# A 1-core decoder layer: first norm from a features-first copy of the tokens, gating bias on ScalarE, and other SBUF places around the output projection

## The chip, the core and the metric

The kernel runs on one core of a Trainium2 chip. The metric is the device time of one execution in microseconds (us). Engines are named as in the profile: PE (TensorE, matmul), PEld (its weight loads), DVE (VectorE), ACT (ScalarE), POOL (GpSimd), SP (SyncE, which here only issues DMA transfers).

## What is computed

One layer of a decoder serves a prompt group of 512 tokens and a sample group of 64 tokens (8 sequences of 8), with D = 1024:

```python
z = rmsnorm(x, ln1_g) @ w_in            # q, kv (4 streams), window kv, gates, u|v
o_a = nsa_mixer(q, kv, window, gates)   # compressed + selected + window attention
o_b = gelu(u) * (w_s @ layernorm(gelu(v)) + b_s)   # per 128 positions, w_s lower triangular
h = x + concat(o_a, o_b) @ w_out
y = rmsnorm(h + relu(rmsnorm(h, ln2_g) @ w_ff1)**2 @ w_ff2, ln_f_g)

def rmsnorm(x, g):
    y = x * rsqrt(mean(x * x, axis=-1) + EPS)
    return y * g
```

The prompt group attends to itself. Each sample sequence attends to a paged cache of 1024 earlier positions and to 512 window rows, which a page table and a state array supply. The new key, value and window rows are outputs too, and so is the window state shifted by 8 rows.

## The kernel before, in words

All matrix products run in float32r with both operands split in a high and a low part (`split`, L104 to L107: ACT copies the high part, DVE or POOL subtracts it to get the low one). A product is then three products (high by high, high by low, low by high). The 64 sample tokens stand as high and low part beside each other in one 128-column operand (`AST`, `Hst`), so that two products are enough. `load_unit` (L136 to L141) loads 128 x 512 of a weight matrix into a `raw` tile and splits it into a unit `wu`. Tokens come in five tiles: t = 0 to 3 are the prompt's, 128 rows each, t = 4 is the sample's 64 rows.

The program is staged, and a tile framework orders each engine's instructions by priorities and dependences; SP issues all DMA transfers in one order, and a transfer behind a waiting one waits with it. The stages and their place in the profiled span:

- **First norm and key/value projection**, 0 to 45 us (L306 to L328). For each token tile: load the rows, sum of squares (ACT), inverse root `rstd` (DVE and POOL, L143 to L148), scaled rows `xn` (DVE), eight PE transposes through PSUM, a split into `AH` and `AL`; for the sample tile into `AST`. Then 24 products of that tile (16 for the sample) into one PSUM bank `pd`, over the eight units of `w_in` columns 512 to 1023, and its evacuation `ev_kv` (L260).
- **Gating values and compressed keys**, 45 to 78 us: columns for v, five banks side by side, and the compression of the prompt's keys (`pc`).
- **Window keys, gates, spatial gating, queries**, 78 to 120 us. `psg` (L489 to L494) holds the mixed values; DVE adds the bias `bsc` out of PSUM, four times 128 x 512. `wsT` is copied out of PSUM by DVE (L455). `evac_q` (L506 to L521) scales the queries by 0.125 and splits them to `Q`, ACT and DVE straight from PSUM.
- **Prompt attention**, 120 to 240 us, with query (`pq`) and u (`pu`) products as filler between its steps.
- **Sample attention**, 240 to 354 us, in four pairs of sequences, 0 to 3. A pair's 16 cached pages (16 x 256 KB) are a tile `G` (`load_pages`, L624). For a pair: compressed keys (`pcs`, PE products over `G`), window scores (`w_a`, `w_b`), selected scores (`s`), the softmax on ACT and DVE (`soft`), compressed values (`pcs` again), and then the values (`values`: transposes `tp` of the probabilities, products `o` over `VB`, `G` and `W`, a last transpose `to`). `values` of a pair runs inside the next pair's turn. There are three buffers for four pairs: pair 3's pages are loaded into pair 0's buffer as soon as pair 0's values have been formed (`load_pages(3, gps[0])` at `pr == 1`, L917). After that SP issues eight copies of window state to the output, HBM to HBM (`out_wins`, L926).
- **Output projection and second norm**, 354 to 422 us: the attention result `OTp` (features first) is split into `Hh` and `Hl`, 16 units of `w_out` are loaded and split, `out_proj` (L970 to L983) forms t = 0 to 3 for each half of the columns and then the sample tile, the result is added to the residual `R[t]`, and `norm_transpose` (L150) makes the next operand. The places in SBUF for `Hh`, `Hl`, `raw` and the units (pools L931 to L947) lie over the tiles of the sample attention, and the five PSUM banks of `acc` over its banks.
- **FFN**, 422 to 810 us, and the last norm to 829 us.

## Time and profile before

| what | value |
|---|---|
| device time, median of 3 runs | 832.47 us (831.67 to 832.74) |
| the profiled execution, its own time | 831.24 us |
| its span | 829.0 us |
| busy PE, DVE, ACT, POOL | 793.0, 444.6, 347.2, 175.0 us |
| mean PE clock granted | 0.991 of full speed |

An engine's busy time is the time in which it had an instruction in work; waits and DMA issues are not counted. The span is the profiled stretch, 2.2 us less than the time of that execution. A line of the chain of work names what the end of the program waited for at that moment, followed back from the last instruction. "<-DVE xn" in an idle time's brackets says who ended it.

### The profile page before, as it was taken

The page shows a single profiled execution, that of the slowest core. Times are in us where ns is not written, and L with a number is a line of the kernel's source. Part 1 is how long each engine was busy: PE and PEld are TensorE (multiplying, and loading weights), DVE is VectorE, ACT ScalarE, POOL GpSimd, SP SyncE. Part 2 cuts the span into 40 slices and gives each one's busy share as a digit, 9 for nine tenths or more (in the row PEclk, how much of TensorE's full clock was granted, in tenths as well). Part 3 has the DMA queues.
Part 4 walks back from the last instruction along what each step waited for, and adds up shares of the span by engine and source line. Part 5 has one row for each costly group of instructions (what it writes and reads, how often), then busy time and mean ns, then how long its engine had stood idle before and what let it go on. Part 6 is the DMA issues. An engine that isn't in the chain of part 4 may idle for free.

```text
span 829.0 us, 13177 instructions
## 1 busy us (share of the span) xinstructions
PE 793.0 (96%) x4855; PEld 687.2 (83%) x4855; DVE 444.6 (54%) x972; ACT 347.2 (42%) x856; POOL 175.0 (21%) x219
## 2 busy tenths in 40 slices
PE   5999999999999999799999999999999999999996
PEld 4788978878776777578888998989989899898985
DVE  4553978899864423474746245163452634435325
ACT  5444467888753232451734242242322323232213
POOL 2001844454210011140212010111111111111112
PEclk9999999999999999999999999999999999999998
DMA  8561420100698167193334132141320413302003
GB/s 265 169 194 35 127 62 14 39 2 1 235 334 271 43 213 226 30 284 118 119 111 141 64 99 63 44 153 51 102 88 15 154 51 102 102 16 99 1 1 114
DMA packets 54178, 90.20 MB, mean 109 GB/s; under 512 B 7618, under 2 KB 18850, under 8 KB 53986
## 3 DMA queue, kind: packets, MB, share of 16 engines
q1 hardware_dynamic: 53858, 89.30, 34.0%
q8 instruction: 38, 0.62, 0.3%
q14 instruction: 26, 0.21, 0.1%
q0 software_dynamic: 256, 0.07, 0.0%
HBM read 85.08 MB, written 8.39 MB: 113 GB/s over the span
## 4 chain that ended last, share of the span: by engine, by line
PE 85%; DVE 5%; DMA 3%; ACT 3%; issue 1%; SPq 1%; POOL 1%; POOLq 0%; ACTq 0%; DVEq 0%
PE acc L95 52%; PE pd L95 7%; PE pcs L95 6%; PE o L95 4%; PE pu L95 3%; PE s L95 3%; PE tp L685 2%; PE pq L95 2%; DMA raw<-in_w_in 2%; PE pc L95 1%; DVE wu L107 1%; DVE y L1034 1%; DMA G<-in_cache_kv 1%; ACT Hh L106 1%; ACT wu L106 0%
## 5 line engine op out<-in xcount | busy, mean ns | idle before, releaser
L95 PE MATMUL acc<-Hh,wu 128*128 128x288 f32 x1024 | 206.0, 296 | 0.0
L106 ACT ACTIVATE wu<-raw 128x512 fp32r<-128x512 f32 (+1 forms) x184 | 105.9, 614 | 157.8 <-PE acc L95 119.7
L95 PEld LDWEIGHTS acc<-Hh,wu 128*128 128x128 f32 x1024 | 165.3, 189 | 0.6 <-ACT Hh L106 0.2
L95 PE MATMUL acc<-wu,Fh 128*128 128x512 f32 x512 | 155.5, 389 | 0.0
L95 PE MATMUL acc<-Hl,wu 128*128 128x288 f32 x512 | 151.2, 296 | 0.0
L107 DVE TENSOR_TENSOR wu<-raw,wu 128x512 fp32r<-128x512 f32 x160 | 110.2, 730 | 53.5 <-ACT wu L106 53.5
L95 PEld LDWEIGHTS acc<-wu,Fh 128*128 128x128 f32 x512 | 95.7, 188 | 19.5
L95 PE MATMUL acc<-wu,Fl 128*128 128x512 f32 x256 | 97.1, 389 | 0.0
L95 PEld LDWEIGHTS acc<-Hl,wu 128*128 128x128 f32 x512 | 96.4, 188 | 0.3
L1055 DVE TENSOR_TENSOR f<-relu 128x576 f32<-128x576 f32 x32 | 24.2, 756 | 118.8 <-ACT relu L1054 118.8
L958 DVE TENSOR_TENSOR R<-acc,R 128x512 f32<-128x512 f32 x72 | 47.6, 687 | 62.8 <-PE acc L95 62.6
L1054 ACT ACTIVATE relu<-acc 128x288 f32<-128x288 f32 x64 | 26.1, 408 | 117.8 <-PE acc L95 117.8
L964 POOL TENSOR_TENSOR R<-atm,R 64x512 f32<-64x512 f32 x18 | 30.5, 1701 | 155.0 <-DVE atm L963 148.6
L1057 POOL CAST Fst<-Fh 128x64 fp32r<-128x64 f32 x32 | 23.5, 734 | 176.5 <-ACT Fh L106 119.7
L95 PE MATMUL pcs<-G,w 128*128 128x256 f32 x256 | 58.9, 383 | 0.0
L95 PEld LDWEIGHTS acc<-wu,Fl 128*128 128x128 f32 x256 | 48.1, 188 | 10.1
L95 PE MATMUL pd<-wu,AH 128*128 128x512 f32 (+1 forms) x192 | 55.7, 373 | 0.7 <-ACT wu L106 0.5
L95 PEld LDWEIGHTS pcs<-G,w 128*128 128x128 f32 x256 | 47.3, 190 | 9.7 <-issue 3.6
L661 ACT ACTIVATE P<-s,nm 128x32 f32<-128x32 f32 (+4 forms) x88 | 40.2, 463 | 9.9 <-DVE nm L660 9.5
L107 POOL TENSOR_TENSOR wu<-raw,wu 128x512 fp32r<-128x512 f32 (+1 forms) x24 | 30.1, 1271 | 57.7 <-ACT wu L106 53.9
L95 PE MATMUL acc<-wu,Hh 128*128 128x512 f32 x128 | 40.7, 403 | 0.1
L95 PEld LDWEIGHTS pd<-wu,AH 128*128 128x128 f32 x192 | 34.1, 191 | 7.0 <-ACT wu L106 0.9
(318 smaller groups left out, 1336.2 us busy)
## 6 DMA issues: line engine op xcount, KB each, us to landing
raw<-in_w_ff SPq DMA_DIRECT2D x128, 256.0 KB
G<-in_cache_kv SPq DMA_DIRECT2D x64, 256.0 KB
raw<-in_w_in SPq DMA_DIRECT2D x32, 256.0 KB
raw<-in_w_out SPq DMA_DIRECT2D x16, 256.0 KB
out_wins<-in_state_win_kv SPq DMA_DIRECT2D x8, 504.0 KB
KW<-in_win_kt SPq DMA_DIRECT2D x4, 512.0 KB
W<-in_state_win_kv SPq DMA_DIRECT2D x8, 256.0 KB
R<-in_x_prompt SPq DMA_DIRECT2D x4, 512.0 KB
```

The lines of the kernel that those rows point to most:

```text
L95: pe.matmul(out, lhsT, rhs, start=start, stop=stop, skip_group_check=not first_in_bank)
L106: act.activation(hi, src, AF.Copy)
L107: eng.tensor_tensor(lo, src, hi.bitcast(F32), op=ALU.subtract)
L661: act.activation(p_[:, c0:c0 + w], src, AF.Exp, bias=nm[:, br, g:g + 1], accum_out=l[:, br, g:g + 1])
L685: pe.transpose(t_[:w, g * 128:(g + 1) * 128], P[g][:, c0:c0 + w], ident)
L958: dve.tensor_tensor(R[t][:, c0:c0 + 512], p, R[t][:, c0:c0 + 512], op=ALU.add)
L964: pool.tensor_tensor(R[4][:, c0:c0 + 512], tm2, R[4][:, c0:c0 + 512], op=ALU.add)
L1034: dve.scalar_tensor_tensor(y[:rows], R[t], r[:rows], gf[:rows], op0=ALU.mult, op1=ALU.mult)
L1054: act.activation(r[:, i * 288:i * 288 + 288], p[:, :288], AF.Relu)
L1055: dve.tensor_tensor(f2, r, r, op=ALU.mult)
L1057: pool.tensor_copy(Fst[:, m, 0:64], Fh[:, m, 512:576].bitcast(F32))
```

## The change

Four parts.

1. **Start.** The host hands over a second, features-first copy of the tokens, `x_t` (8 x 128 x 576), and `ln1_g` in columns. `AH` and `AL` are made from it with the gain alone (ACT and DVE, one 128 x 576 step each for every k), without the row's inverse root; there are no transposes. The projection runs k by k over four banks at once, the sample's 16 products last. The token rows are loaded as well, later, for the sum of squares alone. The inverse root `rs[:, t, 0]` (and half of it) is multiplied in at every evacuation: as the scale of ACT's copies, in `gelu`, by one more DVE step in `halves`. For the queries, whose tokens are columns, five products `prb` spread it over all partitions into `rb`, and `evac_q` multiplies by that (a DVE step `qf`), then splits from SBUF.
2. **Gating.** The bias is added by ACT (8 steps of 128 x 256) in place of DVE's four; `wsT` is copied by ACT in place of DVE.
3. **Places.** `Hl` and three units' places now lie on SBUF's other side, opened before the sample attention. `Hh` and `raw` lie exactly on pair 0's `G`, other small tiles on pair 1's, `fwb` on pair 2's. The residual rows are loaded into `OTp`'s own place, when `OTp` has been split.
4. **Pages of pair 3** go into pair 1's buffer, after pair 1's values (`pr == 2`), in place of pair 0's at `pr == 1`.

```diff
+        for k in range(8):
+            xt = n1.tile([128, NT], F32, name="xt", tag="xt", bufs=4)
+            sp.dma_start(xt, I["x_t"][:, k])
...
+            act.activation(AH[:, k], xt, AF.Copy, scale=g1c[:, k:k + 1])
+            dve.scalar_tensor_tensor(AL[:, k], xt, g1c[:, k:k + 1], AH[:, k].bitcast(F32), op0=ALU.mult, op1=ALU.subtract)
+            us.append(load_unit((wp, wp0)[k % 2], w_in[k * 128:(k + 1) * 128, 512:1024], 512))
...
+        for k in range(8):
+            for t in range(4):
+                tok_step(ps_[t], t, k, us[k], 512)
+        for k in range(8):
+            tok_step(ps_[4], 4, k, us[k], 512)
+        sp.dma_start(cst, I["consts"][:, :NKEEP])
...
         for t in range(5):
...
+            sp.dma_start(x[:rows], xin[t])
...
+            act.activation(q[:rows], x[:rows], AF.Square, accum_out=ss[:rows])
+            r = rstd_of(n1, ss, D, rows)
...
+            ev_kv(t, ps_[t])
...
+            mm(prb[t // 4][:, (t % 4) * 128:(t % 4) * 128 + rows], bcast(rs[:rows, t, 0:1], [[0, 128]]), ident[:rows, :rows],
...
+        act.activation(rb[:, 0:512], prb[0], AF.Copy, scale=0.125)
...
+            act.activation(wsT[:, g2 * 4:g2 * 4 + 4, :], p, AF.Copy)
...
-            dve.tensor_tensor(S[:, 0:4, g * 64:g * 64 + 128].rearrange("p t (g c) -> p g t c", g=2), p,
-                              bcast(bsc[:, g:g + 2], [[1, 2], [0, 4], [0, 64]]), op=ALU.add)
+            for e in range(2):
+                act.activation(S[:, 0:4, (g + e) * 64:(g + e) * 64 + 64], p[:, e], AF.Identity, bias=bsc[:, g + e:g + e + 1])
...
+        qf = ev.tile([128, 288], F32, name="qf", tag="qf", bufs=2)
+        dve.tensor_tensor(qf, p[:, :288], rb[:, half * 288:half * 288 + 288], op=ALU.mult)
...
-                if pr == 1:
-                    load_pages(3, gps[0])
+                if pr == 2:
+                    load_pages(3, gps[1])
...
+    R = [OTp[:, 2 * t:2 * t + 2].rearrange("p a c -> p (a c)") for t in range(4)] + [fb.tile([64, D], F32, name="R4")]
...
```

How this moves instructions. On PE, at the start of the program (`ptr` are the transposes of the first norm, `pd` the projection's products), the order before:

```order
L172 MATMUL ptr<-cst,xn 128x128 x8
L95 MATMUL pd<-wu,AH 128x512 x2
L95 MATMUL pd<-wu,AL 128x512
L95 MATMUL pd<-wu,AH 128x512 x2
L95 MATMUL pd<-wu,AL 128x512
L95 MATMUL pd<-wu,AH 128x512
L172 MATMUL ptr<-cst,xn 128x128 x8
```

and the changed kernel's, at the end of the same stage:

```order
L95 MATMUL pd<-wu,AL 128x512
L95 MATMUL pd<-wu,AH 128x512 x2
L95 MATMUL pd<-wu,AL 128x512
L95 MATMUL pd<-wu,AST 128x512 x16
L95 MATMUL prb<-cst,rs 128x128 x4
L95 MATMUL prb<-cst,rs 128x64
L371 MATMUL ppos<-cst,posr 128x32
```

The products now stand first on PE, without a transpose; the five `prb` products, which need every row's inverse root, stand behind them and ahead of all later PE work.

On PE, in pair 2's turn of the sample attention (L889 and L894 are the `tp` transposes of L875 and L880 before, L914 is L900), before:

```order
L95 MATMUL o_3949<-G,PT 64x128 x16
L95 MATMUL pv_3918<-w2z,gsq 64x64 x4
L95 MATMUL pcs<-G,w_2619 128x256 x5
L95 MATMUL o_3949<-W,PT 64x128 x8
L95 MATMUL pcs<-G,w_2619 128x256 x10
L900 MATMUL to<-cst,ob 128x128
L95 MATMUL pcs<-G,w_2619 128x256
L875 MATMUL tp_4122<-cst,P_3843 80x128
L880 MATMUL tp_4125<-cst,P_3843 128x128 x4
```

and in the changed kernel:

```order
L95 MATMUL o_3903<-G,PT 64x128 x16
L95 MATMUL pv_3872<-w2z,gsq 64x64 x4
L95 MATMUL o_3903<-W,PT 64x128 x8
L914 MATMUL to<-cst,ob 128x128
L889 MATMUL tp_4127<-cst,P_3797 80x128
L894 MATMUL tp_4130<-cst,P_3797 128x128 x4
L894 MATMUL tp_4137<-cst,P_3797 128x128 x4
L894 MATMUL tp_4144<-cst,P_3797 128x128 x4
L95 MATMUL pcs<-G,w_2617 128x256 x16
L95 MATMUL pk_4027<-gsq,w2z 128x128 x2
L95 MATMUL pcs<-G,w_2617 128x256 x10
```

The 16 `pcs` products over pair 3's pages, which stood between the values and the transposes, now stand behind all of them, and no output projection stands there. One pair later, `acc` products of the output projection now stand between the steps of pair 3's values: 25 ahead of `to`, 93 ahead of the last `to`; before, all of them stood behind it.

On SP the changed kernel issues, ahead of pair 3's pages (`G`):

```order
L136 DMA raw<-in_w_out 128x512 x7
L1003 DMA OTp<-in_x_prompt 128x1024
L620 DMA W<-in_state_win_kv 128x4x128 x2
L136 DMA raw<-in_w_out 128x512
L1003 DMA OTp<-in_x_prompt 128x1024
L136 DMA raw<-in_w_out 128x512
L1003 DMA OTp<-in_x_prompt 128x1024
L776 DMA VB<-out_wins 8x2x128
L777 DMA VB<-out_kvs 8x2x128
L940 DMA out_wins<-in_state_win_kv 16x8064 x2
L351 TENSOR_LOAD ptt
L635 DMA G<-in_cache_kv 128x512
```

Before, the eight `out_wins` copies and all `w_out` loads stood behind the 16 page loads; now two of the copies and ten of the loads stand ahead of them.

## Rows read from the trace of the kernel before

**Rows 1.** The page, part 1: busy us, share of the span, instructions.

```profile
PE 793.0 (96%) x4855; PEld 687.2 (83%) x4855; DVE 444.6 (54%) x972; ACT 347.2 (42%) x856; POOL 175.0 (21%) x219
```

**Rows 2.** Windows by stage: stretch, length; busy us (instructions) per engine, PE clock, DMA share, GB/s.

```profile
0.00:12.60 12.60, 3.92 (x13) 3.21 (x14) 4.53 (x12) 6.64 (x12) 2.18 (x8) 1.00 0.78 289
12.60:45.10 32.50, 31.09 (x153) 24.20 (x152) 19.17 (x37) 17.11 (x34) 2.88 (x7) 1.00 0.65 179
...
97.00:120.00 23.00, 22.03 (x161) 20.19 (x159) 18.01 (x46) 9.97 (x32) 13.56 (x16) 1.00 0.42 113
...
304.90:330.06 25.16, 24.05 (x171) 18.88 (x171) 10.28 (x38) 7.74 (x25) 2.08 (x1) 1.00 0.58 187
330.06:354.10 24.04, 16.67 (x167) 12.47 (x166) 9.94 (x37) 11.38 (x32) 5.89 (x5) 0.92 0.16 46
354.10:400.00 45.90, 45.90 (x204) 37.86 (x205) 27.79 (x38) 15.28 (x30) 9.61 (x8) 0.97 0.52 171
```

**Rows 3.** Waits of PE over the whole span: total us, times, longest.

```profile
PE ptr L172 <- DVE xn L167: 8.7, 1, 8.7
```

**Rows 4.** Timeline of the start: start us, us, engine, line, operation.

```profile
4.07 0.63 ACT L158 ACTIVATE xn<-x 128x512 f32<-128x512 f32 x1 [2.06 <-DMA x<-in_x_prompt]
...
8.59 1.29 ACT L106 ACTIVATE wu<-raw 128x512 fp32r<-128x512 f32 x2 [2.13 <-DMA raw<-in_w_in]
...
8.69 1.97 PE L172 MATMUL ptr<-cst,xn 128*128 128x128 f32 x8 [8.69 <-DVE xn L167]
...
10.56 1.22 PE L95 MATMUL pd<-wu,AH 128*128 128x512 f32 x2
```

**Rows 5.** The chain of waits, three pieces around 45 us: start us, us.

```profile
40.97 3.74 PE pd L95 x16
...
44.71 0.33 PE pkc L394 x3
...
45.37 12.18 PE pd L95 x52
```

**Rows 6.** Groups by form, 100 to 160 us: busy us, mean ns of one.

```profile
L514 DVE SCALAR_TENSOR_TENSOR Q<-pq,Q 64x288 fp32r<-64x288 f32 x8 | 3.6, 454 | 0.7 <-ACT Q L513 0.5
...
L493 DVE TENSOR_TENSOR S<-psg,bsc 128x512 f32<-128x512 f32 x4 | 2.8, 692 | 1.3 <-PE psg L95 1.2
```

**Rows 7.** Timeline of SP's issues, 287 to 318 us.

```profile
287.78 9.53 SPq L628 DMA_DIRECT2D G<-in_cache_kv  x16
...
311.89 5.50 SPq L926 DMA_DIRECT2D out_wins<-in_state_win_kv  x8
```

**Rows 8.** Windows of the sample attention, columns as in the stages above.

```profile
288.00:302.00 14.00, 12.89 (x78) 10.51 (x77) 5.60 (x17) 4.58 (x13) 2.11 (x1) 1.00 0.92 316
...
312.00:330.00 18.00, 16.89 (x112) 13.95 (x108) 6.76 (x20) 4.57 (x13) 2.08 (x1) 1.00 0.81 260
...
340.10:343.50 3.40, 0.00 (x0) 0.00 (x0) 2.48 (x10) 1.74 (x6) 0.77 (x1) 0.99 0.00 0
343.70:347.10 3.40, 3.40 (x19) 2.56 (x18) 0.29 (x1) 1.20 (x2) 1.11 (x1) 0.54 0.02 5
...
353.90:357.40 3.50, 3.42 (x9) 2.47 (x9) 3.32 (x2) 2.34 (x5) 3.50 (x4) 0.55 1.03 294
```

**Rows 9.** Timeline of PE: pair 2's turn, then the end of pair 3's.

```profile
310.94 1.92 PE L95 MATMUL o<-G,PT 128*64 128x128 f32 x32
...
316.63 4.58 PE L95 MATMUL pcs<-G,w 128*128 128x256 f32 x20
...
324.67 0.71 PE L95 MATMUL pk<-gsq,w2z 128*128 128x128 f32 x4
325.22 4.91 PE L95 MATMUL pcs<-G,w 128*128 128x256 f32 x22
...
343.52 0.43 PE L875 MATMUL tp<-cst,P 128*80 128x128 f32 x1 [3.45 <-DVE P L103]
...
353.58 0.43 PE L900 MATMUL to<-cst,ob 128*128 128x128 f32 x1 [3.44 <-ACT ob L898]
```

More of the change, by code (lines that the diff above doesn't have):

```diff
@@ L210, in _body @@
     w_in = I["w_in"][0]
+    rs = inp.tile([128, 5, 2], F32, name="rs")
+    rb = inp.tile([128, NT], F32, name="rb")
+    g1c = inp.tile([128, 8], F32, name="g1c")
     def tok_step(p, t, k, u, n):
@@ new lines, in _body @@
+        act.activation(AST[:, :, 0:64], AH[:, :, 512:576].bitcast(F32), AF.Copy)
+        dve.tensor_copy(AST[:, :, 64:128], AL[:, :, 512:576].bitcast(F32))
+        ps_ = [psm.tile([128, 512], F32, name="pd", tag="mm") for t in range(5)]
+        for k in range(8):
[4 more added lines that the diff above has]
+        sp.dma_start(cst, I["consts"][:, :NKEEP])
+        dve.tensor_copy(identb, ident)
@@ L330, in _body @@
+        prb = [pst.tile([128, 512], F32, name="prb", tag="tr") for _ in range(2)]
+        for t in range(5):
+            rows = tsz[t]
+            mm(prb[t // 4][:, (t % 4) * 128:(t % 4) * 128 + rows], bcast(rs[:rows, t, 0:1], [[0, 128]]), ident[:rows, :rows],
+               t % 4 == 0, True, t % 4 == 0)
+        act.activation(rb[:, 0:512], prb[0], AF.Copy, scale=0.125)
+        act.activation(rb[:, 512:576], prb[1][:, :64], AF.Copy, scale=0.125)
     sp.dma_start(cst2, I["consts"][:, NKEEP:])
@@ L467, in _body @@
             if t == 4:
-                tmp = halves(p, 512)
                 p = ev.tile([64, 512], F32, name="zg", tag="z")
-                dve.tensor_tensor(p, vps[4][0:64], tmp, op=ALU.add)
-            gelu(nc, gw, p, 512, None, None, out=S[:rows, t], rows=rows)
+                halves(vps[4], 512, p)
+            gelu(nc, gw, p, 512, None, None, out=S[:rows, t], rows=rows, scales=rs[:, t] if t < 4 else None)
             st6 = gw.tile([128, 6], F32, name="st6", tag="st6")
@@ L585, in beside @@
                 gelu(nc, uw, p[:, :256], 256, None, None, out=u[:rows], rows=rows,
-                     times=S[:rows, t, hf * 256:hf * 256 + 256])
+                     times=S[:rows, t, hf * 256:hf * 256 + 256], scales=rs[:, t] if t < 4 else None)
                 if prev:
@@ L745, in _body, with tpool @@
     cpq.close()
+    def tpool(name, bufs, **kw):
+        return ctx.enter_context(tc.tile_pool(name=name, bufs=bufs, reuse_waits="tile", **kw))
+    Hl = tpool("fol", 1, side="right").tile([128, 8, NT], F32R, name="Hl")
+    fwa = tpool("fwa", 3, side="right")
     with cs as c3:
@@ L1095, in _body, with gelu @@
                 last_norm(t, t == 3)
-def gelu(nc, pool_, src, n, bias, hbias, out=None, rows=128, times=None):
+def gelu(nc, pool_, src, n, bias, hbias, out=None, rows=128, times=None, scales=None):
     sq = pool_.tile([128, n], F32, name="gsq", tag=f"gsq{n}")
@@ L1102, in gelu @@
     sq, xh = sq[:rows], xh[:rows]
-    if bias is None:
+    if scales is not None:
+        nc.scalar.activation(sq, src, AF.Square, scale=scales[:, 0:1])
+        nc.scalar.activation(xh, src, AF.Copy, scale=scales[:, 1:2])
+    elif bias is None:
         nc.scalar.activation(sq, src, AF.Square)
```

109 lines of the change are left out of this document (39 added, 70 removed).

## The prediction

> **What bounds the kernel now.** I read the page's busy shares first. PE works 793.0 of the span's 829.0 us [rows 1], so only about 36 us can be won without removing PE work; what matters is where those 36 us lie and who causes them. The windows by stage answer that [rows 2]. Three stretches stand out. In the first 12.6 us PE works 3.92. In pair 3's turn of the sample attention (330.06 to 354.10) it works 16.67 of 24.04. Nearly everywhere else it is full: 31.09 of 32.50 in the rest of the first projection, 24.05 of 25.16 in pair 2's turn, 45.90 of 45.90 in the first part of the output projection. The waits of PE name the cause at the start: 8.7 us in one piece for the normalised rows [rows 3]. The timeline of the last pair shows two more: 3.45 us for the probabilities on DVE and 3.44 us for `ob` on ACT [rows 9].
>
> A second cost hides behind each such idle time. The window 340.10 to 343.50 has PE at 0.00 busy; in the next one (343.70 to 347.10) PE is full, at a granted clock of 0.54. After the second idle time the clock is 0.55 [rows 8]. These are the two levels, 2.4 and 1.2 GHz. So a stretch of 3.4 us is worth half, and an idle time of about 3.4 us has a tail of some 1.6 us.
>
> **The change, part by part.** All sums are against the profiled execution, 831.24 us, which lies 1.23 under the median of 832.47.
>
> *Start.* Before, ACT sees its first data at 4.07 us and its first weights at 8.59; PE begins with transposes at 8.69 and with products at 10.56 [rows 4]. The changed kernel loads one 295 KB piece of `x_t` and one weight unit first. From the first use at 4.07, behind about 0.4 MB, and the 289 GB/s of that stretch [rows 2], both have landed by about 4.6 to 5.2; with one split of 0.64 (two take 1.29 [rows 4]) PE starts at about 5.9. Then come 96 + 16 = 112 products. Full speed is 12.18/52 = 0.234 us each [rows 5] (the 16 of the sample take 3.74), so 26.2. The first two of the program take 1.22 instead of 0.47 [rows 4]; PE was new to work from 8.69 to about 12.6, and I charge half of 3.9, that is 2.0. The products end at 34.1. The five `prb` products are not in the trace; from the key transposes (0.11 each [rows 5]) to the first transposes (1.97/8 = 0.25 [rows 4]) they cost 0.6 to 1.2, and I take 1.2, since they are new in that place: 35.3. Before, the next stage begins at 45.37, behind 12 key transposes of 0.11 that in the changed kernel come later: 45.37 - 1.3 - 35.3 = 8.8. I take off 0.3 for the next unit's split, which stands on ACT behind the evacuations: **-8.5**, bounds -9.3 and 0. The bound of 0 is the case in which the row statistics come late (rival C): what ends last is then not a product but the last row load.
>
> *Evacuations and bias.* DVE loses four steps of 0.692 [rows 6] and two `wsT` copies of the same size, 4.2 together; it gains eight `qf` steps at about 0.454 (the nearest row is the 64x288 step of `evac_q` [rows 6]) and three of `halves` at up to 0.69, 5.7 together. ACT gains eight bias steps and two copies, some 4.4, and is busy 9.97 of 23.0 us there [rows 2]. The query evacuation becomes one DVE step longer. PE is idle only 0.97 us in that stretch, and the queries' products have several banks, so the longer evacuation is covered by other products; if that cover is missing, each of the last evacuations costs 0.45. I take **+0.2**, bounds -1 and +2.
>
> *Sample attention, pair 1.* `Hh`'s eight copies and the first units' splits now stand on ACT ahead of pair 1's exponential. That moves the probabilities later by about the splits' 4 to 5 us. The transposes that wait for them stood behind 30 `pcs` instructions that cover most of it: **+1.0**, bounds 0 and +3.4.
>
> *Sample attention, the reload.* This is the costly term. Count from pair 2's `w_a` at 304.90. Before, pair 3's pages were issued at 287.78 [rows 7], a whole pair ahead. Now they are issued when pair 1's values are read, and those end at 310.94 + 1.92, that is +8.0 [rows 9]. Two copies `out_wins` stand ahead of them. Eight copies with two W loads kept the DMA engines busy 0.81 of 18 us, 14.6 [rows 8]; without W (1.7) one is 1.6, two are 3.2. The 16 loads, 4.19 MB, at 316/0.92 = 343 GB/s [rows 8] need 12.2, and with their start and landing about 13. The pages are there at about +24.6. PE has its other work (values, transposes) done by about +17, with an idle time of 3.4 before the transposes as in the last pair [rows 9]. Then it waits some 7.5 us. After that come 32 `pcs` instructions of 0.22 (22 take 4.91 [rows 9]), 7.1; their slow clock, 1.7; the wait for the compressed keys between the last of them and `pk`, about 2.9 (316.63 + 4.58, two more instructions, then 324.67 [rows 9]), which transposes covered before and nothing covers now; `pk`, 0.6; 20 `pcs` instructions, 4.5; and half of a further slow stretch, 0.8. The turn takes about 42.2 instead of 25.16: **+17.0**, bounds +11 and +21.
>
> *Sample attention, the last pair.* `acc` products now fill the waits, 25 of them ahead of the first `to` and 93 ahead of the last. The turn's own work is 16.67 less what the slow clock added (half of 3.4), that is 15.0; it took 24.04, so 9.0 comes back, and 1.6 more because the first `acc` products no longer run at 0.55 [rows 8]: **-10.6**, bounds -11.6 and -5. The earlier loads of `w_out` win nothing more, since PE was full from 354.10 on [rows 2].
>
> *Rest.* The residual in `OTp`'s place and the early `gf` and `g2` loads hide behind a full PE: 0. If that cover fails, late residual rows cost one DVE addition.
>
> Sum: -8.5 + 0.2 + 1.0 + 17.0 - 10.6 = -0.9, so 830.3 for a profile like the one shown and **831.6 us** against the median. I call anything within 0.2% (1.7 us) no change.
>
> **A rule weighed.** The trace gives 343 GB/s for page loads, and I let them wait for the copies [rows 8]. The Trainium skill, DMA: Bandwidth & Descriptors (Bandwidth, Measured), has 341 GB/s at 1 MB and 425 at 16 MB, and the same page (Queues, rings and completion order) says that an engine takes its descriptors in ring order. By its rates the reload takes an estimated 9.9 to 12.3 us, up to 3 us less than I charge, and the sum would be near 829; by its order the copies stay ahead, as I have it. The trace agrees with the lower of the two rates.
>
> **Rivals.** *B, the reload is cheaper than charged.* The loads do not wait for the copies (-3.2) and one slow stretch falls away (-1.8): 831.6 - 5.0 = 826.6. For it: the copies read and write HBM only, and the loads' rate was taken in company of other work. Against it: one queue. Chance 0.31.
>
> *C, the row statistics come late.* PE's `prb` products stand ahead of everything that follows, and need the sample rows' inverse root. Those rows are the last of some 8.7 MB on one queue; behind them come a square and a root, about 2 us. At 289 GB/s [rows 2] they land at 32 and the root is ready at 34.2, just when PE needs it; at 316 [rows 8] at 31.6. From a landing after 32 on, each microsecond costs one. The mean over both windows of the start is 210 GB/s [rows 2], which eats the whole gain; at 250 GB/s the delay is about 4.7: 836.3, slower. For it: 12.60 to 45.10 shows only 179 GB/s. Against it: that queue was not kept full. Chance 0.16.
>
> *D, PE is clocked down through the whole reload.* Pair 2's turn has three idle times in a row (probabilities, pages, compressed keys). If each is followed by a slow stretch as in rows 8, that is 1.7 for the first, 0.8 more for the last, and a DMA queue behind one more W load, 1.7: +4.2, 835.8. [...] The Trainium skill, TensorE: Matmul & The Clock Gate (Part 1), calls the throttled clock the default that activity releases; rows 8 agree with 0.54 and 0.55 after two idle times. Chance 0.14.
>
> *E, the change does not do what it says.* `acc` products stand beside the last pair, but the units they read must be split by ACT between that pair's own steps. If they come late, half of the 10.6 is lost: 836.9. Chance 0.06.
>
> **How the numbers follow.** My forecast has 0.33, and its time is the prediction. Faster: B and a little of the forecast's spread, 0.36; slower: C, D and E with hardly any of it taken off, 0.35; no change 0.29. For the range I take in B to 826.0 and C to 838.0; what lies beyond (the copies free and no slow stretch at all; the start's gain lost entirely) has about 0.2. The forecast's own range is 829.9 to 833.3.
>
> **What would show it.** After: first PE product near 6 us, next stage (the 52 products) near 36.6; if C, an idle PE ahead of `prb`. Pair 2's turn near 42 us with one PE idle time of 7 to 8 us ended by DMA `G`; if B, under 38. Pair 3's turn near 15 us of its own work with `acc` between, and no half clock behind it. FFN and last norm unchanged to 0.5 us. If pair 2's turn stays at 25 us, or pair 3's at 24, my picture of the reload or of the filling is wrong.

## The result, and the profile after

The changed kernel takes 844.5 us (median of 4, 842.3 to 845.99), the kernel before on the same chip 832.07 (median of 4, 831.54 to 832.74). The ratio is 1.0147, with a 95% interval of 1.0122 to 1.0172: **slower by 12.4 us**. The forecast was 831.6, with a range up to 838. A repeat on another chip gave 844.09 against 833.28.

The profiled execution of the changed kernel has a span of 840.5 us, 11.5 more than before. The page, part 1, of the changed kernel, to be read against [rows 1]:

```profile
PE 793.6 (94%) x4825; PEld 687.9 (82%) x4825; DVE 441.5 (53%) x980; ACT 353.9 (42%) x864; POOL 177.4 (21%) x219
```

PE's busy time is the same to 0.6 us, though there are 30 fewer PE instructions. So the 11.5 us are in sum new idle time (10.9), and the question is where it lies. The busy time hides a second loss behind the saved transposes: the mean granted clock is 0.982 in place of 0.991. The windows of the changed kernel, one per stage (the sample attention cut where each pair's first `w_a` product stands, so the four rows from 254.63 on are pairs 0, 1 and 2 and the first part of pair 3), to be read against [rows 2]:

```profile
45.00:97.00 52.00, 48.70 (x313) 43.16 (x312) 33.66 (x71) 24.86 (x58) 19.76 (x16) 1.00 0.44 119
...
254.63:277.94 23.31, 19.92 (x104) 14.78 (x104) 10.79 (x35) 7.35 (x21) 2.35 (x2) 0.93 0.59 204
277.94:308.78 30.84, 26.62 (x171) 20.69 (x171) 16.89 (x41) 13.37 (x36) 13.57 (x10) 0.89 0.55 189
308.78:351.16 42.38, 27.68 (x174) 21.65 (x173) 10.41 (x38) 8.00 (x25) 2.08 (x1) 0.80 0.59 210
351.16:365.00 13.84, 13.84 (x119) 10.72 (x119) 9.83 (x30) 7.29 (x20) 0.00 (x0) 1.00 0.09 27
```

In the kernel before, the `w_a` of the four pairs stand at 257.06, 279.74, 304.90 and 330.06. A table of the marks splits the whole difference without a remainder:

| stretch | before, us | after, us | difference | forecast |
|---|---|---|---|---|
| start of the program to pair 1's `w_a` | 279.74 | 277.94 | -1.8 | -8.3 |
| pair 1's turn | 25.16 | 30.84 | +5.7 | +1.0 |
| pair 2's turn (the reload) | 25.16 | 42.38 | +17.2 | +17.0 |
| pair 3's `w_a` to the end | 498.94 | 489.34 | -9.6 | -10.6 |
| sum | 829.0 | 840.5 | +11.5 | -0.9 |

The two large terms came out nearly as forecast. Two terms that were thought to be settled, the start and pair 1, miss by 6.5 and 4.7 us.

The longest waits of PE in the changed kernel (engine, tile, line, what it waited for: total us, times, longest), to be read against [rows 3]:

```profile
PE pcs L95 <- DMA W<-in_state_win_kv: 8.6, 1, 8.6
PE tp L889 <- DVE P L103: 8.6, 3, 3.4
PE pd L95 <- ACT wu L106: 7.1, 2, 6.7
PE pk L95 <- DVE gsq L1130: 3.4, 2, 2.3
```

`tp` waits for the probabilities in pairs 0, 1 and 2 now; before it did once, in pair 3 (3.45 [rows 9]). The wait in pair 3 is gone.

**The start, and where its gain went.** Timeline of the changed kernel's start on PE, against [rows 4, 5]:

```profile
6.65 2.50 PE L95 MATMUL pd<-wu,AH 128*128 128x512 f32 x5 [6.65 <-ACT wu L106]
...
34.81 1.41 PE L95 MATMUL prb<-cst,rs 128*128 128x128 f32 x10
36.33 1.42 PE L95 MATMUL pd<-wu,AH 128*128 128x512 f32 x5
```

The next stage begins at 36.33 in place of 45.37 [rows 5], 9.0 earlier; 7.7 of it is left when the 12 key transposes (about 1.3) that now come later are taken off. 8.5 of it was forecast. But the first query product (`pq`) is only 4.1 earlier (95.4 before, 91.3 after), the last score product of the prompt attention 4.5 earlier (235.0 and 230.5), and pair 1 only 1.8. The window from 45 to 97 shows the first loss: PE is idle 3.30 us there (52.00 - 48.70), against 0.19 in the same stretch before, of which this is the window:

```profile
45.00:97.00 52.00, 51.81 (x319) 46.02 (x318) 29.32 (x62) 24.46 (x59) 16.39 (x14) 1.00 0.39 108
```

Two causes stand in that stretch. Weights and other loads come late around 51 to 54 us (three waits, 1.2 together, all of them gone in e10 below); PE's chain of waits goes over a weight load there, which lands at 50.31 and is split before PE can go on, where before the chain stayed on PE [rows 5]. From the changed kernel's chain (start us, us):

```profile
36.46 13.85 DMA raw<-in_w_in
```

And PE waits for ACT ahead of the queries (0.46 for `wsT`, 1.34 for `th`, the gates' tanh). Then PE, in the changed kernel, waits for DVE at the end of the prompt attention and in pair 0: `pk` 1.08, `w_b` 1.29, `tp` 1.81. Behind the last one the clock is at half for a while (0.93 over pair 0's turn, 1.00 in that of the kernel before). That turn is 0.6 us longer than before although eight `pcs` instructions more stand ahead of it (64 in place of 56).

One profile isn't enough to size this. Ten profiles show this start and the new gating with the token rows (the changed kernel's and nine of those below). Up to pair 0 all ten have the same order on PE, ACT, DVE and POOL, and yet pair 0's `w_a` lies between 254.05 and 259.22. Their means lie off those of three profiles with the old start and gating (the kernel before's two and e2's) by -4.5 at the first `pq`, -3.5 at the last score product, -1.4 at pair 0's `w_a` and -1.4 at pair 1's. So the gain melts in the mean too.

**Pair 1.** The same stretch in the kernel before and after. Timeline of DVE in the kernel before, from the exponential's sum to the scaled probabilities:

```profile
291.65 0.17 DVE L863 TENSOR_SCALAR r<-l 128x2 f32<-128x2 f32 x1 [1.31 <-ACT P L860]
291.86 0.17 DVE L864 RECIPROCAL r<-r 128x2 f32<-128x2 f32 x1
292.06 0.16 DVE L865 TENSOR_TENSOR r<-r,gts 128x2 f32<-128x2 f32 x1
292.25 0.89 DVE L103 TENSOR_SCALAR P<-P,r 128x8 f32<-128x8 f32 x2
```

Timelines of ACT, POOL, DVE and PE in the changed kernel, the same steps:

```profile
286.39 4.27 ACT L106 ACTIVATE Hh<-OTp 128x512 fp32r<-128x512 f32 x8 [1.81 <-DMA VB<-out_kvs]
...
291.08 1.14 ACT L874 ACTIVATE P<-P,nm 128x1032 f32<-128x1032 f32 x1
...
287.10 10.87 POOL L107 TENSOR_TENSOR Hl<-OTp,Hh 128x512 fp32r<-128x512 f32 x8 [7.50 <-ACT Hh L106]
...
292.57 1.24 DVE L877 TENSOR_SCALAR r<-l 128x2 f32<-128x2 f32 x1
293.85 0.17 DVE L878 RECIPROCAL r<-r 128x2 f32<-128x2 f32 x1
294.05 0.98 DVE L879 TENSOR_TENSOR r<-r,gts 128x2 f32<-128x2 f32 x1
...
295.56 2.97 DVE L103 TENSOR_SCALAR P<-P,r 128x8 f32<-128x8 f32 x2
...
298.58 0.43 PE L889 MATMUL tp<-cst,P 128*80 128x128 f32 x1 [3.35 <-DVE P L103]
```

ACT does `Hh` ahead of the exponential, as forecast. What was not: while POOL works at `Hl` (287.10 to 297.97), small DVE steps grow by about 1 us each. `r<-l`, two numbers per partition, goes from 0.17 to 1.24; `r<-r,gts` from 0.16 to 0.98; the scaling of `P` from 0.89 to 2.97. The reciprocal between them stays at 0.17. Counted from the turn's own `w_a`, the exponential begins 2.5 us later than before (13.14 against 10.63) and the probabilities are ready 7.2 later (20.59 against 13.40): 2.5 ahead of the exponential, nearly all of it ACT's splits, 4.0 from the three steps that grew, 0.7 from weight splits that stand between them on DVE. PE's other work lasts until 295.23, that is 17.29, so it could have hidden 3.9 of the 7.2. The other 3.3 are its wait, and behind that the clock falls. Windows of the changed kernel behind that wait (columns as in the stages):

```profile
298.00:302.00 4.00, 2.55 (x10) 1.61 (x10) 3.13 (x10) 0.90 (x2) 2.48 (x1) 0.51 0.98 370
302.00:305.50 3.50, 3.50 (x13) 3.06 (x13) 0.00 (x0) 0.96 (x2) 0.00 (x0) 0.58 0.23 92
```

POOL's own part of the scaling is late too (297.95, behind `Hl`), but the transposes that read it come only in the next turn, so nothing waits for it. The turn's +5.7 is idle time for 3.1 (30.84 - 26.62 = 4.22, against 1.11 in pair 2's turn before [rows 2], which is as long as pair 1's) and the half clock for 2.6 (26.62 busy in place of 24.05).

**Pair 2, the reload.** Timelines of SP and PE in the changed kernel, against [rows 7, 9]:

```profile
317.49 1.24 SPq L940 DMA_DIRECT2D out_wins<-in_state_win_kv  x2
...
320.03 9.27 SPq L635 DMA_DIRECT2D G<-in_cache_kv  x16
...
322.63 0.43 PE L889 MATMUL tp<-cst,P 128*80 128x128 f32 x1 [3.40 <-DVE P L103]
322.86 2.99 PE L894 MATMUL tp<-cst,P 128*128 128x128 f32 x12
334.43 9.43 PE L95 MATMUL pcs<-G,w 128*128 128x256 f32 x32 [8.59 <-DMA W<-in_state_win_kv]
346.20 0.71 PE L95 MATMUL pk<-gsq,w2z 128*128 128x128 f32 x4 [2.33 <-DVE gsq L1130]
```

The `pcs` products read `G`, not `W`; the profile names whatever landed last before they began, and the same wait in another kernel's trace is put down to `G` (below). PE is idle 3.40 + 8.59 + 2.33 + 0.38 = 14.70 us in this turn. Windows of that wait and of the first products behind it:

```profile
328.00:333.00 5.00, 0.00 (x0) 0.00 (x0) 0.00 (x0) 0.00 (x0) 0.00 (x0) 0.50 1.05 393
333.00:338.00 5.00, 3.57 (x8) 2.86 (x9) 0.00 (x0) 0.00 (x0) 0.00 (x0) 0.50 1.23 436
```

Nothing at all works from 328 to 333 but the DMA engines: this is what a transfer on the path looks like. In the repeat (e12, below) this turn takes 43.5.

### The profile page after: what moved, and what is told of

The parts are those of the page before. It is cut to its first block, busy times and chain, and to the rows that moved or that the text cites. A ratio compares the mean times of both kernels' runs of the same rounds, so it can differ in the third digit from the quotient of the medians.

```text
span 840.5 us, 13155 instructions
## 1 busy us (share of the span) xinstructions
PE 793.6 (94%) x4825; PEld 687.9 (82%) x4825; DVE 441.5 (53%) x980; ACT 353.9 (42%) x864; POOL 177.4 (21%) x219
## 4 chain that ended last, share of the span: by engine, by line
PE 81%; DVE 6%; DMA 4%; ACT 3%; issue 2%; POOL 1%; SPq 1%; POOLq 0%; ACTq 0%; DVEq 0%
PE acc L95 53%; PE pcs L95 6%; PE pd L95 5%; PE o L95 4%; PE pu L95 3%; PE pq L95 3%; PE s L95 2%; PE tp L692 2%; DMA raw<-in_w_in 2%; PE pc L95 1%; POOL wu L107 1%; DVE Q L522 1%; ACT P L668 1%; DMA G<-in_cache_kv 1%; DMA W<-in_state_win_kv 1%
## 5 line engine op out<-in xcount | busy, mean ns | idle before, releaser
L107 DVE TENSOR_TENSOR wu<-raw,wu 128x512 fp32r<-128x512 f32 x160 | 105.2, 695 | 45.7 <-ACT wu L106 45.6
L972 DVE TENSOR_TENSOR OTp<-acc,OTp 128x512 f32<-128x512 f32 x72 | 47.7, 686 | 63.5 <-PE acc L95 63.4
L95 PE MATMUL pcs<-G,w 128*128 128x256 f32 x256 | 63.1, 403 | 8.6 <-DMA W<-in_state_win_kv 8.6
L95 PEld LDWEIGHTS pcs<-G,w 128*128 128x128 f32 x256 | 50.8, 203 | 19.7 <-DMA G<-in_cache_kv 9.0
```

Source lines behind the costliest of these rows:

```text
L95: pe.matmul(out, lhsT, rhs, start=start, stop=stop, skip_group_check=not first_in_bank)
L107: eng.tensor_tensor(lo, src, hi.bitcast(F32), op=ALU.subtract)
L972: dve.tensor_tensor(R[t][:, c0:c0 + 512], p, R[t][:, c0:c0 + 512], op=ALU.add)
```

## The experiments

Each kernel ran on a chip beside the kernel before, whose medians there were 833.3 to 833.7 us. Ratios are against that.

**The change in its halves.** The first kernel (e1) keeps parts 1 and 2 and takes back the places and the pages; its core:

```diff
-                if pr == 2:
-                    load_pages(3, gps[1])
+                if pr == 1:
+                    load_pages(3, gps[0])
...
-    R = [OTp[:, 2 * t:2 * t + 2].rearrange("p a c -> p (a c)") for t in range(4)] + [fb.tile([64, D], F32, name="R4")]
+    R = [None] * 4 + [fb.tile([64, D], F32, name="R4")]
```

> Parts 1 and 2 of the change alone, on the places and the page order of the kernel before. In the changed kernel pair 0's first window product began at 254.63 in place of 257.13, so the start is worth 2.5 us there, not the 8.5 forecast. Theory (the rest is given back before the sample attention, whatever the places): about 829.6, the first window product near 254.6. Rival (the places took the rest away, since they move fillers or loads of the prompt attention): 824 to 826, first window product near 249.

Measured: 831.58 us, ratio 0.9976 (0.9961 to 0.999). The start with the gating is worth 2.0 us (0.24% of 833), not 8: nearer to the theory than to the rival, which fell. The second kernel (e2) is the other half: the kernel before with parts 3 and 4 alone (the pages at `pr == 2` from `gps[1]`, and the new places).

> Parts 3 and 4 alone, with the start and the gating of the kernel before. Theory (the loss lies in pair 1's turn, +5.7, and pair 2's turn, +17.2, and 9.6 come back behind pair 3's start): 832.1 + 13.3 = 845.4, pair 2's turn near 42 us. Rival (the turns grow only because the start made the earlier work run closer to its loads): pair 2's turn under 38 us, time under 841.

Measured: 846.76 us, ratio 1.0151 (1.0124 to 1.0179). Pair 1's turn is 30.67, pair 2's 44.05, near the theory's. So the whole loss is in parts 3 and 4, and within the intervals the halves add up: -0.24% and +1.51%, against +1.47% for both.

**What the start is worth, and why not more.** Part 1 alone (e1b, the gating as in the kernel before):

> Part 1 alone (the start), without the bias and the transposes' copies on ACT. Theory (what eats the start's 9 us is DVE's and ACT's work ahead of the first query product, in which the bias has no place, and the end of the prompt attention): the first query product near 91 to 92 and pair 0's first window product within 1 us of that of parts 1 and 2 together; time 831 to 833.5. Rival (the bias and the copies on ACT hold up the evacuations that PE waits for, 1.3 us ahead of the first query product): 1 to 2 us earlier from there on, time 829 to 831.

Measured: 834.65 us, 1.0012 (0.9995 to 1.0028), no change, and above both forecasts; the first `pq` is where the theory put it. The kernel before was profiled on the same chip beside it:

> The kernel before, profiled on the chip of these runs, so that stage times can be set side by side. Every theory expects the stages of the trace shown, to about 1 us: next stage of the projection from 45.4, first query product at 95.4, first prompt score at 119.5, first window product of pair 0 at 257.1.

Measured: 832.44 us, one run. The marks of the two show the gain melting: the first `pq` at 91.4 against 96.2 (-4.8), the first score product over window keys at 116.5 against 120.3 (-3.8), the last at 233.0 against 235.8 (-2.8), pair 0's `w_a` at 258.62 against 257.86 (+0.8). Part 2 alone (e2b) is two edits in the kernel before:

```diff
-            dve.tensor_copy(wsT[:, g2 * 4:g2 * 4 + 4, :], p)
+            act.activation(wsT[:, g2 * 4:g2 * 4 + 4, :], p, AF.Copy)
...
-            dve.tensor_tensor(S[:, 0:4, g * 64:g * 64 + 128].rearrange("p t (g c) -> p g t c", g=2), p,
-                              bcast(bsc[:, g:g + 2], [[1, 2], [0, 4], [0, 64]]), op=ALU.add)
+            for e in range(2):
+                act.activation(S[:, 0:4, (g + e) * 64:(g + e) * 64 + 64], p[:, e], AF.Identity, bias=bsc[:, g + e:g + e + 1])
```

> Part 2 alone (bias and transposes' copies on ACT) on the kernel before. In the run with the old start, part 2 and early pages, pair 0's first window product came at 265.6, against 257.8 in the run with the places alone. Theory (with the old start, part 2 moves the query and u products in the order of the prompt attention, and loses there): first window product near 265, time 838 to 841. Rival (the places with early pages, which begin loads and pools in the prompt attention, lose it, not part 2): first window product near 257 to 258, time 832 to 834.

Measured: 838.05 us, 1.0051 (1.0025 to 1.0076): slower alone, though on top of the new start it brings some 3 us (1.0012 to 0.9976). Pair 0's `w_a` stands at 260.63, between the 265 of the theory and the 257 to 258 of the rival. What differs widely ahead of it is the order in which the framework lays out the prompt attention. From 160 to 200 us PE is busy 38.45 of 40 us at a clock of 0.96 here, and 39.88 at 1.00 in the kernel before. That the order does it is argued, not shown; why it tips this way stays open.

Next, the load queue (e10). In e1's kernel the token rows, their squares and their roots were taken out; the rows' inverse root is the constant 1, so that part of the computation is left out:

```diff
-            x = n1.tile([128, D], F32, name="x", tag="x")
-            sp.dma_start(x[:rows], xin[t])
...
-            act.activation(q[:rows], x[:rows], AF.Square, accum_out=ss[:rows])
-            r = rstd_of(n1, ss, D, rows)
-            dve.tensor_copy(rs[:rows, t, 0:1], r[:rows])
-            dve.tensor_scalar(rs[:rows, t, 1:2], r[:rows], 0.5, None, op0=ALU.mult)
+            dve.memset(rs[:rows, t, 0:1], 1.0)
+            dve.memset(rs[:rows, t, 1:2], 0.5)
```

> Parts 1 and 2 on the old places, without the token rows, their squares and roots: the row factor is the constant 1, so the row's inverse root is left out of the result. 2.3 MB of loads and five squares fewer. Theory (ahead of the first query product the start's gain is eaten by the load queue, which is full from 36 to 54 us, so that weights come late): the first query product, at 92.0 with the rows, comes at 89 or earlier and PE has no wait for weights near 51. Rival (DVE and ACT, at work without a pause from 78 to 96, hold it): it stays at 91 to 92.

The window of that kernel over the stretch in which the weights of the next stage are loaded:

```profile
36.00:54.00 18.00, 18.00 (x94) 15.15 (x93) 8.51 (x18) 6.95 (x15) 0.00 (x0) 1.00 0.70 201
```

The same window of e1, which differs by the rows and their statistics alone, and of the kernel before:

```profile
36.00:54.00 18.00, 16.45 (x77) 13.20 (x77) 7.32 (x18) 7.39 (x18) 0.00 (x0) 1.00 1.00 250
```

```profile
36.00:54.00 18.00, 18.00 (x86) 14.22 (x85) 11.50 (x22) 9.77 (x19) 0.00 (x0) 1.00 0.80 209
```

With the 2.3 MB of rows the DMA engines are at 1.00 and PE waits for weights; without them they are at 0.70 and PE is full. The first `pq` comes at 89.8 in place of e1's 92.0 (the ten kernels with rows: 90.7 to 92.0), so the queue costs about 1 to 2 us there. Pair 0's `w_a` comes at 255.82 in place of 257.92, but that lies within the spread of the ten. Total: 830.84 us, one run, 0.7 under e1's median and inside the range of its runs; that the 2 us reach the end is not shown. The other waits (`pq` for ACT's `th`, 1.3; `w_b`, 1.3) are the same, so the rest of the lost gain is not the queue's.

**Pair 1: what slows the probabilities.** The low part `Hl` is formed on DVE in place of POOL (e3):

```diff
-        split(Hh[:, k, 0:512], Hl[:, k, 0:512], OTp[:, k], pool)
+        split(Hh[:, k, 0:512], Hl[:, k, 0:512], OTp[:, k])
```

> The changed kernel with the eight low parts Hl formed by DVE instead of POOL. Theory (POOL at work beside DVE slows DVE's steps of pair 1's softmax: its scaling took 2.97 us there and 1.28 before; so the transposes wait 3.35): DVE's steps return to their former durations, pair 1's turn falls from 30.8 to about 26 or 27, total 840 to 842. Rival (what delays the softmax is ACT, which copies Hh and splits units ahead of the exponential): pair 1's turn stays at 30 or more, or grows, since DVE now has 5.5 us of work more ahead of the softmax; total 844 or more.

Timelines of DVE and PE of that kernel:

```profile
292.50 4.29 DVE L107 TENSOR_TENSOR Hl<-OTp,Hh 128x512 fp32r<-128x512 f32 x7
...
299.45 1.32 DVE L103 TENSOR_SCALAR P<-P,r 128x8 f32<-128x8 f32 x2
...
300.82 0.43 PE L889 MATMUL tp<-cst,P 128*80 128x128 f32 x1 [2.55 <-DVE P L103]
```

Measured: 843.73 us, 1.0108 (1.008 to 1.0136). The scaling is back to 1.32, so POOL's company was what made it 2.97; but seven `Hl` steps (4.29) now stand ahead of it on DVE, the wait only falls to 2.55, and pair 1's turn is 28.58: some 2 us of the 5.7 come back, less than the theory's 4 to 5. The cause of the slow steps is shown, the cure is not one.

In e11 `Hh` stands behind the exponential on ACT, and `Hl` on DVE behind DVE's last step of the turn (`ends` and `tail` hold those two instructions of each pair):

```diff
-        split(Hh[:, k, 0:512], Hl[:, k, 0:512], OTp[:, k], pool)
+        with tc.issue_after(ends[1]), tc.issue_after(tail[1]):
+            split(Hh[:, k, 0:512], Hl[:, k, 0:512], OTp[:, k])
```

> The changed kernel, late pages and all, with Hh issued behind pair 1's exponential and Hl formed by DVE behind its last step ahead of pair 2's compressed keys. Theory (pair 1's 30.8 in place of 25.2 come from the splits that stand ahead of the softmax or beside it): pair 1's turn falls to 25 to 27, pair 2's stays near 42, total 3 to 5 us under the changed kernel, 839 to 842. Rival (the splitting of units and the new transfers slow pair 1): it stays at 28 or more.

Measured: 841.24 us, 1.0096 (1.0071 to 1.0121); pair 1's turn is 28.45. Timeline of PE of that kernel, pairs 1 and 2:

```profile
296.50 0.33 PE L915 MATMUL to<-cst,ob 128*128 128x128 f32 x1 [1.73 <-ACT ob L913]
...
333.54 9.49 PE L95 MATMUL pcs<-G,w 128*128 128x256 f32 x32 [8.13 <-DMA G<-in_cache_kv]
```

The turn misses the theory's 25 to 27 and keeps the rival's mark of 28, though not by the rival's cause alone. The probabilities are no longer late. `ob` (the copy of the values' result out of PSUM) is: it stands behind `Hh`'s copies on ACT. One wait was traded for a smaller one, and half of the term stays. (Here the trace names `G` for the reload's wait.)

**The reload: do the copies ahead of the pages count?** In the changed kernel the eight window copies are put behind the page loads on SP's queue (e4; `last_g` is the last page load):

```diff
+        with tc.issue_after(last_g[0].ins):
             for b in range(8):
                 tc.keep_in_program_order(sp.dma_start(
```

> The changed kernel with the first two window copies issued behind pair 3's page loads instead of ahead of them. Theory (the loads wait for the copies on one queue, 1.6 us each): PE's wait for the pages falls by about 3.2, pair 2's turn from 42.4 to about 39, time 841 to 842. Rival (the copies, memory to memory, share the engines and delay the pages little): pair 2's turn stays within 1 us of 42.4, time 844 to 845.

Measured: 839.72 us, 1.0073 (1.0049 to 1.0097), with pair 2's turn 40.12 and the wait for the pages 6.6:

```profile
335.90 8.73 PE L95 MATMUL pcs<-G,w 128*128 128x256 f32 x32 [6.60 <-DMA W<-in_state_win_kv]
```

The changed kernel and this one were then run again, side by side on one chip (e12 and e13):

> The changed kernel on the chip of these runs, for the comparison with the next one: 843 to 846, pair 1's turn near 30.8, pair 2's near 42.4.

> The two window copies behind the page loads, on the same chip as the changed kernel. Its first run had pair 2's turn at 40.1 and a median 6 us over before, where the changed kernel had 12.4 on another chip. Theory (the copies hold up the pages by about 2 us and nothing else differs): 2 to 3 us under the changed kernel here. Rival (they cost 6): 5 to 7 us under it.

Measured: the changed kernel 844.09 us, 1.013 (1.009 to 1.0169), pair 2's turn 43.5; with the copies behind 840.12 (9 runs, 837.67 to 844.22), 1.0084 (1.0062 to 1.0106). The profiled execution of the latter, at 842.99 one of its longer ones, has a turn of 44.0 and a wait of 7.8. The medians put the two copies at 4 us, the forecast at 3.2; the intervals overlap and the traces of two executions of one kernel give 40.1 and 44.0. In the traces of e12 and e13, counted from pair 2's `w_a`, the first page load is issued 1.3 us earlier without the copies, and the first product on the pages comes 0.4 earlier. So the size isn't settled. Either way most of the 17 is not the copies.

**The pages early again, with the new places kept.** The changed kernel (e6), but pair 3's pages go into pair 0's buffer at `pr == 1` as before; `Hh` and `raw` then have to lie on pair 1's buffer, so the pools are opened in another order:

```diff
-                if pr == 2:
-                    load_pages(3, gps[1])
+                if pr == 1:
+                    load_pages(3, gps[0])
...
-    Hh = tpool("foh", 1).tile([128, 8, NT], F32R, name="Hh")
-    pools['wraw'] = tpool("wraw2", 7)
-    fw2a = tpool("fw2a", 6)
-    fw2b = tpool("fw2b", 2)
-    fw2 = [fw2a] * 6 + [fw2b] * 2
...
-    tpool("gap", 1).tile([128, 64], F32, name="gap")
+    fw2a = tpool("fw2a", 6)
+    fw2b = tpool("fw2b", 2)
+    fw2 = [fw2a] * 6 + [fw2b] * 2
+    tpool("gap", 1).tile([128, 32], F32, name="gap")
+    Hh = tpool("foh", 1).tile([128, 8, NT], F32R, name="Hh")
+    pools['wraw'] = tpool("wraw2", 7)
```

> The changed kernel with pair 3's pages loaded into pair 0's buffer after pair 0's values, as in the kernel before; Hh and the raw tiles lie on pair 1's buffer instead, and the small tiles, gf and g2 on pair 0's. Theory (the late pages are the whole +17.2 of pair 2's turn, and the output projection can fill pair 3's waits all the same): pair 2's turn falls from 42.4 to between 25 and 31 (it now holds Hh and Hl, which slowed pair 1's turn by 5.7), pair 1's turn from 30.8 to 25, pair 3's tail as in the changed kernel: 826 to 829, faster than both. Rival (the pages are not the limit, but the transposes and compressed keys that follow each other without filler): pair 2's turn stays over 34, total over 835.

Measured: **826.81 us, 0.9919 (0.9896 to 0.9942): faster than both kernels**. Pair 1's turn is 25.60, pair 2's 28.20, and pair 3's `w_a` stands at 331.00 (330.06 before). From there to the end it takes 492.6 us, 6.3 less than before; the fill beside the last pair is kept without the late pages. The rest is 3.3 longer than the changed kernel's 489.34, and that is not the fill: from pair 3's `w_a` to the end of the second norm's transposes the two take 82.4 (e6) and 83.0. It is the FFN, 402.8 to its last product in place of 398.7, with PE full at full clock in both but fewer products in the same time. Windows of 100 us in the FFN of the changed kernel, then of e6:

```profile
534.14:634.14 100.00, 100.00 (x596) 91.24 (x595) 44.48 (x68) 30.89 (x59) 14.95 (x20) 1.00 0.26 84
```

```profile
513.38:613.38 100.00, 100.00 (x588) 90.14 (x587) 44.61 (x68) 30.96 (x59) 14.51 (x20) 1.00 0.25 79
```

The products of 512 columns start 232 ns apart in place of 227, and so they do in e7, e8 and e9, which share e6's places. Places in SBUF are what differs there; which of them costs the 4 us is not shown. Timelines of DVE, POOL and PE in pair 2's turn, into which `Hh` and `Hl` have moved:

```profile
317.78 2.96 DVE L103 TENSOR_SCALAR P<-P,r 128x8 f32<-128x8 f32 x2
...
311.52 10.34 POOL L107 TENSOR_TENSOR Hl<-OTp,Hh 128x512 fp32r<-128x512 f32 x8 [19.18 <-ACT Hh L106]
...
320.79 0.31 PE L889 MATMUL tp<-cst,P 128*80 128x128 f32 x1 [1.14 <-DVE P L103]
```

The slow scaling moved along with POOL's `Hl`: it belongs to that company and not to pair 1. Pair 2's turn is 3 us longer than before. Two kernels tried to take these as well. First, on top of e6, in e7 the split stands behind pair 2's exponential and POOL's own scaling:

```diff
+        with tc.issue_after(ends[2].ins), tc.issue_after(ends[3].ins):
+            split(Hh[:, k, 0:512], Hl[:, k, 0:512], OTp[:, k], pool)
```

> The kernel with pair 3's pages early, and the eight steps of Hh on ACT and of Hl on POOL issued behind pair 2's exponential and its scaling on POOL. Theory (in pair 2's turn of 28.2 the 3 us over the 25.2 of before come from Hh ahead of the exponential, 1.6 us, and from POOL's Hl beside DVE, whose scaling took 2.96 in place of 1.28): pair 2's turn falls to 25 to 26, time 3 us under that kernel, about 823 to 824.5. Rival (the 3 us are PE's slow clock and its order, not the splits): pair 2's turn stays at 28.

Timelines of DVE, POOL and PE of that kernel:

```profile
314.27 0.89 DVE L882 TENSOR_SCALAR P<-P,r 128x8 f32<-128x8 f32 x2
...
319.05 1.31 DVE L1126 TENSOR_SCALAR gsq<-gsq 128x256 f32<-128x256 f32 x1
320.46 1.30 DVE L1127 TENSOR_TENSOR gsq<-gsq,gxh 128x256 f32<-128x256 f32 x1
...
316.48 10.26 POOL L107 TENSOR_TENSOR Hl<-OTp,Hh 128x512 fp32r<-128x512 f32 x8
...
322.49 1.60 PE L899 MATMUL tp<-cst,P 128*128 128x128 f32 x8 [2.73 <-DVE OTs L101]
```

Measured: 828.17 us, 0.994 (0.991 to 0.997), the turn 28.58: the theory as put fell. The scaling is at 0.89 again, but the next DVE steps beside POOL grow in its place (`gsq`, two steps of the GELU on the compressed keys, 0.28 to 1.31 and 0.43 to 1.30), and PE waits 2.73 there. It is not this or that step of the program that is slow; it is whichever step, of the kinds named at the end, stands beside POOL's subtraction. So in e8 `Hl` is formed on DVE, behind the last DVE step of the turn:

```diff
+        with tc.issue_after(ends[2]), tc.issue_after(tail[2]):
+            split(Hh[:, k, 0:512], Hl[:, k, 0:512], OTp[:, k])
```

> The kernel with pair 3's pages early, Hh issued behind pair 2's exponential, and Hl formed by DVE instead of POOL, behind DVE's last step ahead of pair 3's compressed keys. Theory (POOL's Hl beside DVE made DVE's steps there three to four times as long, 0.29 to 1.31 and 0.42 to 1.30, whichever step it met): no DVE step of pair 2's turn is longer than before, the turn falls from 28.2 to 25 to 26 with no half clock, 822 to 825, 3 us under the kernel with pages early. Rival (the turn is long for another reason, its order or the loads beside it): 28 again, no gain.

Timeline of DVE of that kernel:

```profile
318.47 0.89 DVE L103 TENSOR_SCALAR P<-P,r 128x8 f32<-128x8 f32 x2
...
325.27 4.90 DVE L107 TENSOR_TENSOR Hl<-OTp,Hh 128x512 fp32r<-128x512 f32 x8
```

Measured: 827.39 us, 0.9919 (0.9894 to 0.9944). The turn is 25.03, as long as before the change, so the mechanism is settled: e7 and e8 differ only in the engine and place of `Hl`. The total is not better than e6's by anything measurable, and misses the forecast of 822 to 825: pair 0 begins 3 us later in this profile (257.05 against 254.05), with the same code up to there, and what comes behind pair 3's `w_a` is 1.5 longer (494.1). Last, the same kernel with the old start (e9):

> The same with the start of the kernel before (transposes, norm first); the bias on ACT stays. Theory (the new start is worth about 2 us at the end, most of its 9 us are given back): 1 to 3 us over the kernel with the new start. Rival A (in a kernel without late pages the start's gain comes through): 5 to 8 us over it. Rival B (it is worth nothing): within 1 us.

Measured: 831.72 us, 0.9982 (0.997 to 0.9995), 4.3 us above e8, between the theory and rival A. That is the start's worth in a kernel with the gating on ACT; as part 2 without part 1 costs by itself (above), the start has no one price, it has one per order of the prompt attention.

## Why the prediction was wrong

- **The step that failed first is "Start", -8.5.** Its working nearly held up to the place where it stopped: first product at 6.65 (forecast about 5.9), `prb` 1.41 (1.2), and 7.7 of the 8.5 won at the next stage's begin, 36.33. (By the sum itself that stage would begin at 35.6; the 36.6 under the signs doesn't follow from it.) The error was to count the gain at the end of its own stage. The prediction looked at the PE column of the following stages and saw it full, and let PE set the pace there. But DMA was at 0.80 from 36 to 54 us before; with 2.3 MB more and 9 us less time the loads became the limit there (1 to 2 us by e10). Behind that PE waits for ACT and DVE, up to pair 0; these waits are seen in the trace, but no run took them away. By pair 1, 1.8 is left in the profile, 1.4 in the mean of ten; in e1's timed runs, 2.0. The bound of 0 had been set for another reason, late rows.
- **"Sample attention, pair 1", +1.0, bounds 0 and +3.4, measured +5.7.** ACT's splits moved the exponential by 2.5 us (4 to 5 were charged), and the cover was 3.9, so by that working the term would even have been 0. What was missing is a second delay on the next engine: POOL's eight subtractions beside DVE's short steps, which add 4.0 us to a chain of four steps (e3 and e7 show the cause), and the half clock behind the idle time that follows (2.6). The result lies outside the bounds: the term had ended at the step that was moved and had not asked who works beside the step that now comes later.
- **"The reload", +17.0, measured +17.2.** Its parts: values read at +8.4 (forecast +8.0), PE's other work done at +17.1 (+17), the wait 8.6 (7.5), 32 `pcs` 9.4 (8.8), the wait for the compressed keys 2.3 (2.9), the rest 5.0 (5.9). The mechanism held; that the sum fits to 0.2 is luck, since the parts miss by up to 1.1 both ways and the repeat took 43.5. Rival B (cheaper) did not come. The page rate did, 393 GB/s from 328 to 333, above the 343 that was charged; yet the first products on them began at +25.65, about 1 us later than forecast.
- **"The last pair", -10.6, measured -9.6.** PE is full from 351.16 to 365.00 at full clock, with no wait for `to` or `tp`, and no half clock follows. From the end of the second norm to the last product of the FFN it is 398.9 before and 398.7 after, unchanged as forecast. Rival E did not come.
- **Rival C did not come**: PE did not wait ahead of `prb`. **Rival D came in part**: the clock is 0.50 from 324 to 338 and 0.51 to 0.58 in pair 1. Its price was already half in the forecast, and its place was also pair 1, where it had not been looked for.
- The sum of the misses, 6.5 + 4.7 + 0.2 + 1.0 = 12.4, is the distance between -0.9 and +11.5. Neither of the two large misses makes the loss alone: with the start's full gain the kernel would still be 5.0 slower, with pair 1 as forecast 6.8. A start whose gain is given back was only a bound in the prediction and should have been a rival, with the waits of DVE, ACT and the queue in the stages behind it priced one by one.

## What to carry to other kernels

A gain at the beginning counts only as far as the next stage that something else limits: before writing it into the sum, look at the DMA share and at the DVE and ACT columns of the stages behind it, and ask what each of these engines would do if PE came that much earlier. A buffer that is handed on one step later moves a transfer onto the path, and that loss (17 us here) can be sized well from the trace, so look for the arrangement that gives the same places without it, as e6 does. When work is moved onto POOL or past a chain of short DVE steps, look at what stands beside it in time, not only at what stands behind it.

## What the hardware showed

POOL's two-input subtraction in SBUF takes 1.28 us a step; beside it certain DVE steps grow by up to about one such step: 0.17 to 1.24, 0.16 to 0.98, 0.28 to 1.31, 0.43 to 1.30. It goes the other way too: two of the eight steps beside pair 1 took 1.72 and 1.78, each having begun beside a weight split on DVE. The eight, by shortest, median and longest (ns):

```profile
L107 POOL TENSOR_TENSOR Hl<-OTp,Hh x8: 1257/1276/1781, 287.1 to 296.7; 128x512 fp32r<-128x512 f32 x8
```

Other DVE steps are untouched: the reciprocal (0.17 both times) and the reduction over 1032 columns (1.21 both times). The Trainium skill, SBUF — State Buffer (Who interferes with whom), says that a DVE step with two inputs in SBUF, or a copy or `tensor_scalar` in a mode that uses both ports, shares a port pair with POOL, that the one issued second waits for the whole instruction of the other, and that on trn2 a reduction never does. The traces agree in which steps suffer, in the size, up to about one POOL step per wait, and in that either engine can be the one that waits.

While the reload is waited for, the granted clock stays at 0.50, the lower of the two levels, to the end of the wait, and the 32 products behind it take 0.29 us each in the mean (9.43 for all) in place of 0.22 [rows 9]. Behind pair 1's wait of 3.35 us it is 0.51 to 0.58. And the DMA engines moved 393 GB/s from 328 to 333, with the page loads on the queue, from 329.68 on two `W` loads and the first of six copies issued behind them, and no engine at work, against the 343 read from the kernel before.

Kernels with the same instructions in the same order up to pair 0 began it 5 us apart on one chip (254.05 in e6, 259.22 in e3); differences of that size between single profiles of the start are not to be read as effects.
